# A hybrid attention, retention and ConvFFN layer: sums of the down weights, turned rows and gated rows placed earlier

## The chip, the cores and the metric

The kernel runs on one core of a Trainium2 chip. The metric is the device time of one execution in microseconds. Engines are named as in the profile: PE is TensorE (matmuls and transposes), ACT ScalarE, DVE VectorE, POOL GpSimd, SP SyncE, from whose queue nearly all DMAs are issued.

## What is computed

One layer over 1024 latent tokens of 1024 channels, with 256 context tokens. In the reference's words, cut:

```python
hx = _modulate(_rmsnorm(x, norm1_g[l]), sh1, sc1)
(xq, xk, xv, xrq, xrk, xrv, xrg, xga, xgb) = jnp.split(hx @ w_in[l], IN_OFFSETS, axis=-1)
o_na = _na_latent(grid(xq), grid(xk), grid(xv), kc_na, vc_na, na_rpb[l])
o_ret_x, _, _ = _bi_retention(q_r, k_r, _heads(xrv, RET_HEADS), ...)
o_ret = _ret_output(o_ret_x, xrg)
merged = jax.nn.sigmoid(xga) * (o_na @ w_proj_na) + jax.nn.sigmoid(xgb) * (o_ret @ w_proj_ret)
x = x + g1 * (merged @ w_out)
hx2 = _modulate(_rmsnorm(x, norm2_g[l]), sh2, sc2)
x = x + g2 * _conv_ffn(hx2, w_up[l], conv_w[l], conv_b[l], w_down[l])
return _rmsnorm(x, final_norm_g)
```

All is fp32. The modulation values (`sh1` to `g2`) are silu(c) times `w_ada`.

## The kernel before, in words

**Numbers.** Every operand of a matmul is split into a high and a low part: ACT casts the high part (L86), DVE subtracts it from the source (L87), and a product is three matmuls: high by high (L110), high weight by low operand (L111), low weight by high operand (L112). The function `chain` writes them in this order for one output bank; a chain over 512 channels has 12 matmuls, one over 1024 has 24. A weight block of 128x512 is loaded into a ring of three raw tiles (`rawload`, L91) and split into a ring of six tiles `wc`. Gates, up and down use a scheme of Strassen and Winograd on two by two blocks with seven products (`Seven`): sums of the weight blocks are formed first, on POOL or DVE.

**Order.** Instructions are written as Python loops with generators that yield between pieces; a scheduler then puts each engine's instructions in an order, by priorities, but instructions wrapped in `late` keep their program order. What the engines run is fixed before the launch. Each engine works through its own list in order and waits at an instruction until its operands are there; SP does the same with DMAs, so a store that waits for its tile holds all DMAs behind it.

**Stages**, with their place in the profiled span:

1. Start (0 to about 95 us): norms, modulation, first projections.
2. Neighbourhood attention (95 to 397): a loop over 32 units (head pair by row block) with two extra rounds. In each round one unit computes scores and softmax, the one before it transposes its probabilities (bank `ptp`), splits them into `PT` (L496, L504) and multiplies them with the values into `R` (L511), and the one before that is normalised and stored to `d_ona` (L524). `R`'s two halves are added in L514. Beside it, filler pieces on PE are projection chains of the next pair and gate chains. In each round DVE also multiplies one block of `w_ada` (tile `aw`, one buffer, 512 KB) with silu(c) and sums it (L538); its result is used at stage 4.
3. Retention, head by head, with the mixing of the head before as a second stream (397 to 700), and a tail in which the last head is mixed beside three gate chains (`gate_fill`, to 720).
4. Turn and projection of the attention (720 to 773): the rows `d_ona` are loaded as eight raw tiles `onr` of 128 tokens by 512 channels, PE turns them in 32 transposes of 128x128 into banks `tpn` (L1366), ACT copies each bank as high part of `ona` (L1368), DVE subtracts the low part (L1369). Then 16 chains `pn` of 12 matmuls: output block db by token half, `w_pna[db]` against `ona`. In between POOL and DVE form `hx_sums`, sums of normalised input blocks for the gates, split into `hxT`.
5. Gates (773 to 926): eight units `Gates` of seven steps, 12 matmuls a step, interleaved two steps apart (`interleaved`). A finished bank goes through silu or sigmoid (L1484 on ACT), is multiplied with the retention's output or the projected attention on DVE, and stored to `d_orr` (gated rows), `d_pn` or `d_gate`.
6. pr chains (926 to 1024): 16 chains of 24 matmuls, `w_pret[db]` against the gated rows `orr` of one token half. `orr` of half 0 is loaded and split while the last gates run, one block a step from the last unit's first step on (`n0`), and put where `hx` is no longer read (tags of `hxpool`); half 1 is loaded after the gates. The result is multiplied with a gate and added to the projected attention, `sg` (L1600, L1601).
7. Output projection (1024 to 1137), up (to 1551), down (to 1772).

**The sums of the down weights.** `down_sums` forms, for each of 11 blocks j, four sums of the down weights' quarters for stage 7: four loads of 256 KB (`pj`, L1241), four subtracts on POOL (L1249), four stores to `d_w` (L1251). Before, they are spread: five j in the retention (`ret_sums`, one piece per slot, 8 buffers), four in the gates (one piece in three steps), two among the pr chains (7 buffers).

**`gate1`**, the row of the residual's gate broadcast to 128 partitions, is loaded in the middle of stage 6 (`brow`), used in stage 7.

## Time and profile before

| | |
|---|---|
| runs (us) | 1779.46, 1778.84, 1776.31; median 1778.84 |
| profiled execution, its span (us) | 1772.4; the median of the runs is 6.4 longer |
| granted PE clock | 0.991 |
| busy: PE, DVE, ACT, POOL | 97%, 74%, 48%, 32% |
| DMA, moved in all | 261.62 MB, mean 148 GB/s |

The profile has one time for the profiled execution, its span from the first to the last instruction; the runs' times are taken around the whole execution. In the tables `out<-in` names the tiles without their buffer numbers, and a line number is that of the kernel before. A matmul's duration overlaps with that of the next one (0.39 us long, 0.23 us apart), so on PE the distance between two starts is what counts. A value in brackets is the time an engine stood idle ahead of the row, and what it waited for.

### The profile page before, as it was taken

How to read it: one execution, taken by the hardware profiler on the slowest of the kernel's cores; microseconds unless marked ns; L12 is line 12 of the kernel's file. 1: busy time of each engine (PE TensorE's matmuls, PEld its weight loads, DVE VectorE, ACT ScalarE, POOL GpSimd, SP SyncE). 2: the span in 40 equal slices, each digit the busy share in tenths (PEclk: the TensorE clock that was granted, in tenths of full speed). 3: DMA queues.
4: the chain of work that ended last, by engine and by line, in shares of the span. 5: the costliest groups of instructions: out<-in, count | busy, mean ns of one | idle time of the engine just before them, and what ended most of it. 6: DMA issues, size and time to landing. Idle time of an engine off the chain costs nothing.

```text
span 1772.4 us, 24732 instructions
## 1 busy us (share of the span) xinstructions
PE 1725.5 (97%) x8357; PEld 1429.4 (81%) x8357; DVE 1312.3 (74%) x2458; ACT 851.1 (48%) x1833; POOL 570.9 (32%) x477
## 2 busy tenths in 40 slices
PE   8799999999999999999999999999999999999997
PEld 4588888888888888788877888888888888788886
DVE  5978888765776766777655556889899999876755
ACT  5667666652443444443444323454444444554444
POOL 2610000002334343555412400155455555211444
PEclk9899999999999999999999999999999999999999
DMA  9133334432231212677548733742322332586754
GB/s 357 56 113 120 106 113 134 142 110 104 72 108 48 72 39 65 202 243 241 187 168 278 236 127 137 253 147 91 117 90 89 119 119 90 167 297 191 241 167 151
DMA packets 139552, 261.62 MB, mean 148 GB/s; under 512 B 15872, under 2 KB 28320, under 8 KB 139424
## 3 DMA queue, kind: packets, MB, share of 16 engines
q1 hardware_dynamic: 139424, 260.03, 44.3%
q8 instruction: 66, 1.08, 0.3%
q14 instruction: 62, 0.51, 0.1%
HBM read 187.87 MB, written 69.48 MB: 145 GB/s over the span
## 4 chain that ended last, share of the span: by engine, by line
PE 39%; issue 6%; DVE 5%; DMA 3%; POOL 3%; ACT 1%; SPq 0%; POOLq 0%; DVEq 0%; ACTq 0%
PE u L1374 27%; PE y L1374 4%; PE pr L111 2%; PE pr L112 1%; PE pr L110 1%; PE om L123 1%; PE om L122 1%; PE om L121 1%; DMA raw<-d_orr 1%; DVE wc L87 1%; POOL x L1899 0%; DMA uu<-d_t 0%; DMA ur<-in_w_up 0%; DVE b L1350 0%; POOL pd L1936 0%
## 5 line engine op out<-in xcount | busy, mean ns | idle before, releaser
L1374 PE MATMUL u<-T,wc 128*128 128x512 f32 x960 | 225.7, 391 | 0.6 <-ACT pu L1413 0.3
L1374 PE MATMUL y<-wc,ahl 128*128 128x512 f32 x924 | 212.0, 391 | 2.9 <-DVE wc L87 1.8
L1374 PEld LDWEIGHTS u<-T,wc 128*128 128x128 f32 x960 | 179.4, 188 | 41.5 <-ACT pu L1413 4.2
L1374 PEld LDWEIGHTS y<-wc,ahl 128*128 128x128 f32 x924 | 174.4, 189 | 40.2 <-DVE wc L87 2.5
L87 DVE TENSOR_TENSOR wc<-ur,wc 128x512 fp32r<-128x512 f32 x137 | 125.0, 915 | 62.2 <-ACT wc L86 62.2
L86 ACT CAST wc<-ur 128x512 fp32r<-128x512 f32 x137 | 85.1, 622 | 124.3 <-PE y L1374 71.8
L111 PE MATMUL mm<-low,wc 128*128 128x512 f32 (+1 forms) x328 | 124.0, 378 | 0.0
L1374 PE MATMUL u<-h2a,wc 128*128 128x512 f32 x480 | 112.4, 389 | 0.7 <-DVE pu L1422 0.7
L110 PE MATMUL mm<-hx,wc 128*128 128x512 f32 x264 | 107.4, 407 | 0.3 <-DVE vc L221 0.3
L1374 PEld LDWEIGHTS u<-h2a,wc 128*128 128x128 f32 x480 | 90.0, 188 | 19.9 <-DVE pu L1422 1.2
L112 PE MATMUL mm<-hx,wc 128*128 128x512 f32 x264 | 105.1, 398 | 0.0
L86 ACT CAST wc<-s 128x512 fp32r<-128x512 f32 x80 | 49.6, 621 | 89.7 <-PE u L1374 86.9
L123 PE MATMUL mm<-wc,low 128*128 128x512 f32 (+1 forms) x240 | 91.2, 380 | 0.0
L1513 POOL TENSOR_TENSOR col<-col,bcol 128x32 f32<-128x32 f32 x1 | 0.3, 254 | 281.9 <-DVE aw L538 281.9
L1374 PE MATMUL u<-hxT,wc 128*128 128x512 f32 x384 | 89.6, 389 | 0.0
L87 DVE TENSOR_TENSOR wc<-s,wc 128x512 fp32r<-128x512 f32 x80 | 87.3, 1092 | 3.1 <-ACT wc L86 2.6
L1374 PEld LDWEIGHTS u<-hxT,wc 128*128 128x128 f32 x384 | 72.1, 188 | 15.0
L87 DVE TENSOR_TENSOR wc<-raw,wc 128x512 fp32r<-128x512 f32 x92 | 71.4, 784 | 13.3 <-ACT wc L86 13.2
L121 PE MATMUL mm<-wc,hx 128*128 128x512 f32 x192 | 75.2, 392 | 0.6 <-ACT r L1105 0.6
L122 PE MATMUL mm<-wc,hx 128*128 128x512 f32 x192 | 75.2, 392 | 0.0
L86 ACT CAST wc<-raw 128x512 fp32r<-128x512 f32 x92 | 57.0, 622 | 32.3 <-DMA raw<-in_w_up 5.0
L111 PEld LDWEIGHTS mm<-low,wc 128*128 128x128 f32 x328 | 62.1, 189 | 6.9
(393 smaller groups left out, 4695.7 us busy)
## 6 DMA issues: line engine op xcount, KB each, us to landing
ur<-in_w_up SPq DMA_DIRECT2D x80, 256.0 KB, 3.0
ur<-d_a SPq DMA_DIRECT2D x77, 256.0 KB, 3.0
aw<-in_w_ada SPq DMA_DIRECT2D x32, 512.0 KB, 3.3
pj<-in_w_down SPq DMA_DIRECT2D x44, 256.0 KB, 4.9
d_w<-pj SPq DMA_DIRECT2D x44, 256.0 KB, 2.0
d_a<-sa SPq DMA_DIRECT2D x44, 256.0 KB, 2.0
ur<-d_w SPq DMA_DIRECT2D x44, 256.0 KB, 3.5
d_a<-at SPq DMA_DIRECT2D x33, 256.0 KB, 2.7
```

The costliest lines, as they stand in the source:

```text
L86: act.copy(hi, src)
L87: (lo_eng or vec).tensor_tensor(lo, src, hi.bitcast(F32), ALU.subtract)
L110: pe.matmul(out, wh, xh, start=k == 0, stop=False)
L111: pe.matmul(out, wh, xl, start=False, stop=False)
L112: pe.matmul(out, wl, xh, start=False, stop=k == n - 1)
L121: pe.matmul(out, ah, bh, start=first, stop=False)
L122: pe.matmul(out, ah, bl, start=False, stop=False)
L123: pe.matmul(out, al, bh, start=False, stop=last)
L1374: pe.matmul(out, a, b, start=first and n == 0, stop=last and n == 2, skip_group_check=True)
L1513: pool.tensor_tensor(col[:, 16:48], col[:, 16:48], bcol[:, 16:48], ALU.add)
```

## The change

It has three parts.

**Sums.** All 11 blocks of `down_sums` are formed in the attention's loop. The generator is rewritten: six yields per block, asked for twice a round (68 times for 66 yields), with a ring of three `pj` tiles. Each subtract is tied by `with_vec` to the DVE instruction written before it: it starts only when that one has ended. In the order of after, three subtracts of four are tied to an L514, one to an L538. The sums in the retention, the gates and the pr chains are gone.

**Turned rows.** Four of the eight row blocks (token half 0) are loaded, turned and split in the retention's tail, in banks of its own filler chains (`mm_tile`); the other four behind the first pn chain. `ona` is split by halves, half 0 in a pool of its own. The pn chains go (0,0), (1,0), (0,1), (1,1) and then block by block, with the second weight loaded after the first.

**Gated rows.** The loads of `orr` begin six steps earlier in the gates, so that all eight blocks of half 0 and four of half 1 are fetched there; blocks 4 to 7 of half 0 get a pool of their own (`orl`). The first `w_pret` blocks are loaded in the last three steps of the gates. The pr chains go in the same changed order, the last four blocks of half 1 are loaded first in that stage, and then the second block's weights. `gate1` is loaded at the output projection.

PE's order from the retention's last gate chain (`mm`) over the turn (`tpn`) to the first pn chain, before:

```order
L111 MATMUL mm_8349<-low_715,wc_8262 128x512
L112 MATMUL mm_8349<-hx0_119,wc_8262 128x512
L1366 MATMUL tpn_8429<-ident_76,onr_8411 128x128 x4
L1366 MATMUL tpn_8436<-ident_76,onr_8413 128x128 x4
L1366 MATMUL tpn_8443<-ident_76,onr_8415 128x128 x4
L1366 MATMUL tpn_8450<-ident_76,onr_8417 128x128 x4
L1366 MATMUL tpn_8457<-ident_76,onr_8419 128x128 x4
L1366 MATMUL tpn_8464<-ident_76,onr_8421 128x128 x4
L1366 MATMUL tpn_8471<-ident_76,onr_8423 128x128 x4
L1366 MATMUL tpn_8478<-ident_76,onr_8425 128x128 x4
L110 MATMUL pn_8502<-ona0_8409,wc_8499 128x512
L111 MATMUL pn_8502<-ona1_8410,wc_8499 128x512
```

and after, where `ona00` and `ona01` are the high and low part of half 0:

```order
L111 MATMUL mm_8486<-low_715,wc_8399 128x512
L112 MATMUL mm_8486<-hx0_119,wc_8399 128x512
L110 MATMUL pn_8575<-ona00_4591,wc_8572 128x512
L111 MATMUL pn_8575<-ona01_4592,wc_8572 128x512
L1092 MATMUL tpn_8588<-ident_76,onr_8548 128x128 x3
L112 MATMUL pn_8575<-ona00_4591,wc_8572 128x512
L110 MATMUL pn_8575<-ona00_4591,wc_8572 128x512
L111 MATMUL pn_8575<-ona01_4592,wc_8572 128x512
L112 MATMUL pn_8575<-ona00_4591,wc_8572 128x512
L110 MATMUL pn_8575<-ona00_4591,wc_8572 128x512
L111 MATMUL pn_8575<-ona01_4592,wc_8572 128x512
```

The first pn chain now follows the last gate chain directly, and the transposes left are put into and behind it.

ACT's order at the gates' end, before (`c` is a gate's result, `wr` a gate's weight, `raw` of `wc` a weight `w_pret`, `sg` the merge):

```order
L86 CAST orr_10142<-raw_10144 128x512
L1484 ACTIVATE c_10190<-u_9993 128x512
L86 CAST orr_10169<-raw_10171 128x512
L1484 ACTIVATE c_10215<-c_10215 128x512
L86 CAST orr_10196<-raw_10198 128x512
L86 CAST wc_10245<-raw_10243 128x512
L1484 ACTIVATE c_10238<-c_10238 128x512
L86 CAST wc_10250<-raw_10248 128x512
L1570 ACTIVATE sg_10271<-sg_10271 128x512
L86 CAST orr_10274<-raw_10276 128x512
L86 CAST orr_10280<-raw_10282 128x512
L86 CAST orr_10286<-raw_10288 128x512
```

and after, where `u_10073` is the bank that the last unit's fifth step completes, `wc_10269` and `wc_10293` are the first pr chain's weights, `wc_10272` and `wc_10298` those of the last unit's sixth and seventh step, and `wc_10366` (six rows on) the second pr chain's:

```order
L1496 ACTIVATE c_10213<-c_10213 128x512
L1496 ACTIVATE c_10240<-c_10240 128x512
L1496 ACTIVATE c_10263<-u_10073 128x512
L86 CAST orr_10220<-raw_10222 128x512
L86 CAST wc_10269<-raw_10267 128x512
L86 CAST wc_10272<-wr_10059 128x512
L86 CAST wc_10293<-raw_10291 128x512
L86 CAST wc_10298<-wr_10068 128x512
L1496 ACTIVATE c_10287<-c_10287 128x512
L1588 ACTIVATE sg_10332<-sg_10332 128x512
L1496 ACTIVATE c_10313<-c_10313 128x512
L86 CAST orr_10335<-raw_10337 128x512
```

The cast of the first pr weight, which stood behind the last gates' results, now stands ahead of the last two gate weights, and these behind the silu of `u_10073`. PE has the first two pr matmuls ahead of the last unit's sixth step.

SP's order early in the pr stage, before (`raw` from `in_w_pret` the second pr block's weights):

```order
L1566 DMA sg_10322<-d_pn_62 128x512
L91 DMA raw_10294<-d_orr_63 128x512
L1568 DMA sg_10324<-d_gate_61 128x512
L91 DMA raw_10300<-d_orr_63 128x512
L1566 DMA sg_10337<-d_pn_62 128x512
L91 DMA raw_10306<-d_orr_63 128x512
L91 DMA raw_10312<-d_orr_63 128x512
L1568 DMA sg_10339<-d_gate_61 128x512
L91 DMA raw_10318<-d_orr_63 128x512
L1566 DMA sg_10342<-d_pn_62 128x512
L91 DMA raw_10327<-in_w_pret 128x512
L91 DMA raw_10332<-in_w_pret 128x512
```

and after:

```order
L1499 DMA d_gate_61<-c_10287 128x512
L91 DMA raw_10337<-d_orr_63 128x512
L91 DMA raw_10343<-d_orr_63 128x512
L91 DMA raw_10349<-d_orr_63 128x512
L1584 DMA sg_10359<-d_pn_62 128x512
L1499 DMA d_pn_62<-c_10313 128x512
L91 DMA raw_10355<-d_orr_63 128x512
L1586 DMA sg_10361<-d_gate_61 128x512
L91 DMA raw_10364<-in_w_pret 128x512
L91 DMA raw_10369<-in_w_pret 128x512
```

Four loads of half 1 are left ahead of the second pr block's weights instead of eight, and the first three of them stand behind the store of `c_10287`, the result of the last unit's sixth step.

The diff, cut:

```diff
+    def with_vec(ins):
+
+        prev = next(i for i in reversed(nc.cur_bb.bb.instructions) if i.engine == mybir.EngineType.DVE)
+        tc.add_manual_dep(ins.ins, prev.name, mybir.DependencyInfo(mybir.DependencyClass.Sync, mybir.DependencyReason.DATA))
+
+    NH = NF // 2
+
+    def down_sums():
+        def load(j, n):
+            t = na.tile([P, 512], F32, tag="pj", bufs=3, name="pj")
+            sync.dma_start(t, io["w_down"][n % 2, NH * (n // 2) + j])
+            return t
+
+        def minus(o, x, y):
+            with_vec(late(pool.tensor_tensor(o, x, y, ALU.subtract)))
+
+        for j in range(NH):
+            b0, b1 = load(j, 0), load(j, 1)
+            yield
+            b3 = load(j, 3)
+            minus(b0, b1, b0)
+            yield
+            sync.dma_start(d_w[j, 0], b0)
+            minus(b1, b3, b1)
+            yield
+            sync.dma_start(d_w[j, 2], b1)
+            minus(b3, b3, b0)
+            yield
+            sync.dma_start(d_w[j, 1], b3)
+            b2 = load(j, 2)
+            yield
+            minus(b2, b2, b3)
+            yield
+            sync.dma_start(d_w[j, 3], b2)
+
+    sums = down_sums()
...
+        next(sums, None)
...
         if u1:
             u1.values()
+        next(sums, None)
         piece()
         piece()
-    for _ in pieces:
-        pass
+    for it in (pieces, sums):
+        for _ in it:
+            pass
     pna.release()
...
+    onl = sb("ona0", "left")
+    d_onat = d_ona.rearrange("r j c d -> (r j c) d")
+    ona = [[onl.tile([P, NPAIR, 512], F32R, name=f"ona0{w}") for w in range(2)], None]
+
+    def ona_turn(n, raw, tp):
+        for k in range(NPAIR):
+            pe.transpose(tp[:, k], raw[:, k * P : (k + 1) * P], ident)
+        dst = [t[:, :, n % 4 * P : (n % 4 + 1) * P] for t in ona[n // 4]]
+        act.copy(dst[0], tp)
+        vec.tensor_tensor(dst[1], tp, dst[0].bitcast(F32), ALU.subtract)
 
...
-            if i < NCB + NTB - 3 and (head.h == 0 or i >= NCB):
-                next(ret_sums, None)
...
+        n = 0
         for _ in range(RET_FILL):
             g = gate_load()
-            yield from gate_fill(rt, "kz", 2, *g)
+            for _ in gate_fill(rt, "kz", 2, *g):
+                yield
+                if n % 4 == 1 and n // 4 < 4:
+                    ona_turn(n // 4, rawload(d_onat[n // 4 * P : (n // 4 + 1) * P]), mm_tile().rearrange("p (k t) -> p k t", k=NPAIR))
+                n += 1
 
...
-    for n in range(KB):
+    for n in range(4, NTB):
         raw = g_raw("onr")
         sync.dma_start(raw, d_onat[n * P : (n + 1) * P])
         onr.append(raw)
     while stores:
         sync.dma_start(*stores.pop(0))
-    for n, raw in enumerate(onr):
-        tp = pg.tile([P, NPAIR, P], F32, tag="g", bufs=6, name="tpn")
-        for k in range(NPAIR):
-            pe.transpose(tp[:, k], raw[:, k * P : (k + 1) * P], ident)
-        dst = [ona[w][:, :, n * P : (n + 1) * P] for w in range(2)]
-        act.copy(dst[0], tp)
-        vec.tensor_tensor(dst[1], tp, dst[0].bitcast(F32), ALU.subtract)
...
-    hs = None
-    for db in range(KB):
-        if db % 2 == 0:
-            hs = hx_sums(db // 2)
+    hs, wp = None, {}
+    for n, (db, half) in enumerate(((0, 0), (1, 0), (0, 1), (1, 1), *((db, half) for db in range(2, KB) for half in range(2)))):
+        if n % 4 == 0:
+            hs = hx_sums(n // 4)
             next(hs)
-        wp = [wload(io["w_pna"][db, 0])]
-        for half in range(2):
-            sl_ = slice(half * 512, half * 512 + 512)
-            m = g_ps("pn")
-            mm_a(m, wp, lambda k: ona[0][:, k, sl_], lambda k: ona[1][:, k, sl_])
...
-        if db % 2 == 0:
+        if db not in wp:
+            wp[db] = [wload(io["w_pna"][db, 0])]
+        m = g_ps("pn")
+        mm_a(m, wp[db], lambda k: ona[half][0][:, k], lambda k: ona[half][1][:, k])
+        if n == 0:
+            for i, raw in enumerate(onr):
+                ona_turn(4 + i, raw, pg.tile([P, NPAIR, P], F32, tag="g", bufs=6, name="tpn"))
...
+        if n % 4 == 2:
             next(hs)
...
+    orl = sb("orr", "left")
...
+    PLACES = {(0, 0): (1, 0), (1, 0): (0, 0), (1, 1): (0, KH)}
 
     def orr_raw(half, k):
-        i, kb = (k // KH if half else 1 - k // KH), k % KH + KH * half
-        orr[half, k] = [hxpool.tile([P, 512], F32R, tag=f"{t}{i}{kb}", bufs=1, name="orr") for t in ("high", "low")]
+        if (half, k // KH) in PLACES:
+            i, k0 = PLACES[half, k // KH]
+            orr[half, k] = [hxpool.tile([P, 512], F32R, tag=f"{t}{i}{k0 + k % KH}", bufs=1, name="orr") for t in ("high", "low")]
+        else:
+            orr[half, k] = [orl.tile([P, 512], F32R, name=f"orr{t}{k}") for t in range(2)]
         return orr[half, k], rawload(d_orr[k, :, half * 512 : half * 512 + 512], late)
 
-    gate_sums = down_sums(gr, RET_SUMS, GATE_SUMS)
     steps = interleaved(0, len(gu))
-    n0, fetched = steps.index((len(gu) - 1, 0)), None
+    n0, fetched = steps.index((len(gu) - 1, 0)) - 6, None
+    fetches = [(0, k) for k in range(2 * RH)] + [(1, k) for k in range(KH)]
+    wp_next = []
     for n, (i, k) in enumerate(steps):
         gu[i].step(k)
-        if n % 3 == 1:
-            next(gate_sums, None)
         if fetched:
             split(*fetched[0], fetched[1])
             fetched = None
-        if n0 <= n < n0 + 2 * RH:
-            fetched = orr_raw(0, n - n0)
-    wp0 = [wload(io["w_pret"][0, i]) for i in range(2)]
-    for _ in gate_sums:
-        pass
+        if 0 <= n - n0 < len(fetches):
+            fetched = orr_raw(*fetches[n - n0])
+        if n >= len(steps) - 3 and len(wp_next) < 2:
+            wp_next.append(wload(io["w_pret"][0, len(wp_next)]))
...
-    gate1 = wop.tile([P, D], F32, name="gate1")
...
-    pjp = sb("out_sums", "right")
-    out_sums = down_sums(pjp, GATE_SUMS, NH, 7)
     mg = {}
-    wp_next = wp0
-    for db in range(KB):
-        wp = wp_next
-        if db == 0:
-            merge_load(0, (0,))
-            for k in range(2 * RH):
-                hl, raw = orr_raw(1, k)
-                split(*hl, raw)
-            merge_load(0, (1,))
-        if db + 1 < KB:
-            wp_next = [wload(io["w_pret"][db + 1, i]) for i in range(2)]
-            merge_load(db + 1)
-        if db == 2:
-            brow(0, gate1)
-        for half in range(2):
-            m = g_ps("pr")
-            mm_a(m, wp, lambda k: orr[half, k][0], lambda k: orr[half, k][1])
...
-            if db > 1:
-                next(out_sums, None)
-    pjp.release()
+    wps = {0: wp_next}
+    merge_load(0, (0,))
+    for k in range(KH, 2 * RH):
+        hl, raw = orr_raw(1, k)
+        split(*hl, raw)
+    merge_load(0, (1,))
+    for n, (db, half) in enumerate(((0, 0), (1, 0), (0, 1), (1, 1), *((db, half) for db in range(2, KB) for half in range(2)))):
+        nx = 1 if n == 0 else db + 1
+        if nx < KB and nx not in wps:
+            wps[nx] = [wload(io["w_pret"][nx, i]) for i in range(2)]
+            merge_load(nx)
+        m = g_ps("pr")
+        mm_a(m, wps[db], lambda k: orr[half, k][0], lambda k: orr[half, k][1])
...
+    orl.release()
...
+    gate1 = brow(0, op.tile([P, D], F32, name="gate1"))
```

64 lines of the change are left out of this document (19 added, 45 removed).

## The prediction

> **What bounds the kernel now.** The page's first part says which engine to follow.
>
> ```profile
> span 1772.4 us, 24732 instructions
> PE 1725.5 (97%) x8357; PEld 1429.4 (81%) x8357; DVE 1312.3 (74%) x2458; ACT 851.1 (48%) x1833; POOL 570.9 (32%) x477
> ```
>
> TensorE (PE) has work in 97% of the span, and the change leaves its matmuls and transposes the same in number. So it can only win back time in which PE stood still or ran slowly, and only lose by making PE wait. The waits view of PE lists where it stands; of its rows these lie where the change reaches (the larger ones above them are in the start, which it does not touch):
>
> ```profile
> PE pr L110 <- ACT wc L86: 2.8, 1, 2.8
> PE pn L112 <- DVE wc L87: 2.2, 2, 1.5
> PE pr L110 <- ACT orr L86: 2.1, 3, 1.3
> PE tpn L1366 <- DVE ona L1369: 2.1, 1, 2.1
> PE pr L111 <- DVE orr L87: 1.4, 4, 0.7
> ```
>
> The columns are total, number and longest. Sum: 10.6 us, in two places. The windows view cuts the span there (attention; turn of the rows and pn chains; gates; first pr chains). The columns are PE, PEld, DVE, ACT, POOL busy, then the granted clock and the DMA share:
>
> ```profile
> 95.00:397.00 302.00, 301.04 (x1853) 263.88 (x1851) 230.40 (x643) 193.33 (x566) 0.71 (x3) 1.00 0.39 120
> 720.00:773.00 53.00, 48.74 (x222) 40.23 (x221) 49.85 (x61) 29.85 (x53) 30.03 (x20) 0.97 0.60 187
> 773.00:926.00 153.00, 153.00 (x678) 126.57 (x676) 99.08 (x121) 61.25 (x102) 64.15 (x43) 1.00 0.62 208
> 926.00:950.00 24.00, 17.68 (x55) 11.53 (x54) 12.69 (x18) 10.99 (x18) 2.56 (x2) 0.86 0.79 263
> ```
>
> PE is full in the gates and nearly so in the attention; taking GpSimd (POOL) work and DMAs out of the gates frees nothing that ends last. What can be won lies in 720–773 and 926–950, where the clock is below 1 too. The timeline of PE there shows why:
>
> ```profile
> 720.04 2.78 PE L1366 MATMUL tpn<-ident,onr 128*128 128x128 f32 x24
> 724.87 1.87 PE L1366 MATMUL tpn<-ident,onr 128*128 128x128 f32 x8 [2.05 <-DVE ona L1369]
> 726.40 0.77 PE L110 MATMUL pn<-ona,wc 128*128 128x512 f32 x1
> ...
> 925.99 0.39 PE L1374 MATMUL u<-hx,wc 128*128 128x512 f32 x1
> 929.18 0.50 PE L110 MATMUL pr<-orr,wc 128*128 128x512 f32 x1 [2.80 <-ACT wc L86]
> ...
> 932.63 0.63 PE L112 MATMUL pr<-orr,wc 128*128 128x512 f32 x1
> 933.06 0.48 PE L110 MATMUL pr<-orr,wc 128*128 128x512 f32 x1
> 933.38 0.39 PE L111 MATMUL pr<-orr,wc 128*128 128x512 f32 x1
> 933.61 0.39 PE L112 MATMUL pr<-orr,wc 128*128 128x512 f32 x1
> ```
>
> Matmuls of 128x512 start 0.23 us apart (933.38, 933.61), but 0.43 apart (932.63, 933.06) after the gap of 2.80: for about 3.4 us (929.9 to 933.3) PE does half its pace, which costs 1.7 us on top of the gap. After 2.05 us the 8 transposes, 0.116 each before (2.78 over 24), take 1.53 too: the same.
>
> **A: the turn.** Now 32 transposes run at once, and PE waits for the vector engine (DVE) and ScalarE (ACT) to empty their banks: 2.05, plus 1.7 of half pace, plus the 2.2 of the two pn waits: 5.95 us. After it, 16 transposes stand in the retention's tail, the first pn chain follows the last gate chain, and the other 16 stand in and behind that chain. The four evacuations moved into the tail lie on ACT and DVE, with filler chains on PE above them: nothing, and at worst 4 x 0.62. The later pn weights now come one pair ahead, so I let the 2.2 go. But the 32 transposes also covered something:
>
> ```profile
> 720.28 0.59 ACT L360 COPY gs<-mm 128x512 f32<-128x512 f32 x1 [1.06 <-PE mm L112]
> 720.77 0.62 ACT L86 CAST wc<-raw 128x512 fp32r<-128x512 f32 x1
> ...
> 721.42 1.12 DVE L87 TENSOR_TENSOR wc<-raw,wc 128x512 fp32r<-128x512 f32 x1 [5.11 <-ACT wc L86]
> ```
>
> The first pn weight's cast stands on ACT behind the copy of the last gate chain, which ends at 720.04; the order of after keeps that. With the cover gone, PE waits from 720.04 to 721.39 for the high half and a moment to restart (1.45), and for the low half, 722.1 to 722.5, about 0.35 more. Such a gap may or may not bring the half pace (2.05 did); a quarter of 1.7 is 0.4. A: 5.95 - 2.2 = 3.8 us won, bounds 0 (half pace for certain, and the tail's copies all in the open) and 5.95 (no new wait).
>
> **B: the gated rows and first pr chains.** In 926–950 PE issued 55 matmuls, 12.5 us at 0.227; from 926.2, the end of the gates, to 950.2 that is 24.0 for 12.5: 11.5 us lost, to 6.3 of gaps, two stretches of half pace and restarts. What follows the change is set by ACT's and SyncE's (SP) orders, with these prices:
>
> ```profile
> 921.83 0.59 ACT L1484 ACTIVATE c<-u 128x512 f32<-128x512 f32 x1
> 922.32 0.61 ACT L86 CAST orr<-raw 128x512 fp32r<-128x512 f32 x1
> ```
>
> The DMA view of 900–960 has the median from issue to landing in its last column:
>
> ```profile
> raw<-d_orr SPq DMA_DIRECT2D x15, 256.0 KB, 3.4
> raw<-in_w_pret SPq DMA_DIRECT2D x9, 256.0 KB, 4.1
> ```
>
> The half-0 rows are all on chip by the end of the gates, so the waits of today go. Two new ones come. Call E the end of the last unit's fifth step (two steps of 12 matmuls, 2.73 us each, before the gates' end). In the order of after PE then turns to the first pr chain, whose weight ACT casts only behind the silu of that step's bank (it waits for E) and one more row: 0.24 to start as after 720.04, then 0.49 (921.83 to 922.32), 0.52 and 0.62: E+1.9, and the low half of this and the next weight on DVE puts the stall at 2.3. Half pace, at a gap like the 2.05 above, 0.55 x 1.7 = 0.9: **B1** 3.2. Then the second pr chain's weight: its load shares a ring of three with the four rows of half 1, behind them in SP's order, and these stand behind a store of the last-but-one gate, ready at E + 2.3 + 2.73 + 0.9 of pr rows + 0.69 and 0.62 on DVE and ACT = E+7.2. Rows land at E+7.5+3.4 = 10.9; cast, they free a slot at 12.3 and 13.0; the fourth row lands at 15.7, the weight issued at 13.0 at 16.6 to 17.1 and is cast by about 17.4. PE ends the two steps and the first chain (24 x 0.227 = 5.45) at E + 2.3 + 5.46 + 5.45 = 13.2. **B2** 4.2, plus 1.7 of half pace: 5.9. B: 11.5 - 9.1 = 2.4 won; bounds -2.5 (B1 with the full half pace, B2 a landing of 4.1 later) and 11.5 (neither arises). I take the middle way since every step of it has a row.
>
> Under "TensorE: Matmul & The Clock Gate", Part 1, the Trainium skill has the clock halve only when PE is idle for a window of about 3.4 us. By that rule B1, B2 and the turn would cost no half pace, 3.0 us less. The rows differ: half pace follows gaps of 2.05 and 2.80 here; its length of 3.4 us agrees.
>
> **C: the sums in the attention.** 44 loads of 256 KB, 44 stores and 44 subtracts come into the 302 us in which PE has under 1 us free. DMA there is at 0.39, so the 23 MB (76 GB/s on 120) fit; weights are loaded several units ahead, so a slower load costs nothing. SP now stops at each store for the subtract, and the loads of `aw` behind it come later; their product (L538) has no reader before the turn, but stands in DVE's order. Three subtracts of four start with the end of the sum L514, one with that of L538. The timeline of DVE behind an L514 (210.99), in an iteration of the busier half, and the R matmuls on PE that this leads to:
>
> ```profile
> 211.31 1.22 DVE L538 SCALAR_TENSOR_TENSOR aw<-aw,cs 128x1024 f32<-128x1024 f32 x1
> ...
> 212.45 1.46 DVE L496 TENSOR_TENSOR PT<-ptp,PT 128x512 fp32r<-128x512 f32 x2
> ...
> 215.09 0.29 DVE L504 TENSOR_TENSOR PT<-ptp,PT 128x128 fp32r<-128x128 f32 x1
> ...
> 215.78 1.36 PE L511 MATMUL R<-PT,V 128*128 128x256 f32 x10
> ```
>
> DVE has no idle from L538 to L504, whose end (215.38) is 0.40 ahead of R. So a hold above 0.4 reaches PE. What a subtract lasts, and what POOL does to a DVE cast, is in the groups by line (min/median/max; the two rows of L87 are of 95–397, where POOL is idle, and of 926–1024):
>
> ```profile
> L1249 POOL TENSOR_TENSOR pj<-pj x44: 1286/1296/1751, 407.3 to 1014.1; 128x512 f32<-128x512 f32 x44
> L87 DVE TENSOR_TENSOR wc<-raw,wc x31: 671/686/693, 97.8 to 388.2; 128x512 fp32r<-128x512 f32 x31
> L87 DVE TENSOR_TENSOR wc<-raw,wc x21: 674/691/1774, 929.2 to 1023.6; 128x512 fp32r<-128x512 f32 x21
> ```
>
> The worst hold is 1.774 - 0.69 = 1.09 us, the median none. L538 stands ready when L514 ends, while POOL must first be told, so DVE should mostly be first and POOL the one to wait; then L496 to L504 follow, each with one operand in PSUM. Of 32 iterations about 16 run as tight as this one (the others, from 310 on above all, have idle before L484 and L496). One in eight of those 16 holds paying 1.09 - 0.4 = 0.7 is 1.4, and I take 1.5; bounds 0 (a gain is excluded, since no PE wait leaves) and 11 (all 16 pay).
>
> **D: the rest.** Without the subtracts DVE's casts in the retention, the gates and the pr chains run freer; PE waits for none of them in the list above but those priced, so 0.5 won, bounds 0 and 1. The `gate1` row now loads at the out projection's start, where two banks hold the results of two chains meanwhile (2 x 5.45 us against one transfer): nothing.
>
> Sum: -3.8 - 2.4 + 1.5 - 0.5 = -5.2 us. The profiled span of 1772.4 becomes 1767.2; the median of the runs, 1778.84 (1776.31 to 1779.46), lies 6.4 above the span, so the median becomes **1773.6**. A measurement of this kernel can tell about 0.2% (3.6 us) from no change: the forecast, -0.29%, stands just past that. Its own range is 1771 to 1777.
>
> **Rivals.**
> 1. *Held in the softmax's chain (slower).* POOL wins the start, each subtract holds DVE for the full 1.09, and the 16 tight iterations each bring R 0.7 late: 11.2 us; a second subtract (44 in 33 iterations, so 11 of them have two) finds no slack left in the half of these that is tight: 5.5 x 0.4 more = 2.2. -5.2 - 1.5 + 13.4 = +6.7: 1785.5. It decides from a mean hold of 0.8 (0.4 of slack and 6.7/16). For it: PE has no idle to give in 95–397, and the chain above has none. Against: DVE is ready first, and the median cast beside POOL is not held. The Trainium skill's "SBUF — State Buffer", on the port that the two engines share, lets a DVE instruction with two SBUF inputs and a GpSimd one that reads SBUF exclude each other for a whole instruction; the 1.774 agrees, and by this rule L538 and L87, both of that kind, are the wrong neighbours for the sums.
> 2. *The new waits eat the gain (no change).* B1 and A's gap both bring the half pace, and the second weight lands 2 us later: B 2.3 + 1.7 + 6.2 + 1.7 = 11.9, A wins 2.5: +0.4 - 2.5 + 1.0 = -1.1: 1777.7. For it: 2.05 was enough once; the DMA share is 0.79 in 926–950. Against: the pj loads leave that stretch.
> 3. *They do not arise (much faster).* ACT is ahead and the weights lie there: B keeps 2 of 11.5, -3.8 - 9.5 + 1.0 = -12.3: 1766.5. For it: today's last gate weights are cast long before use. Against: the order of ACT and SP, which fixes both waits.
> 4. *New gaps bring no half pace.* -5.2 - 3.0 = -8.2: 1770.6. Against: the slow rows after 2.05 and 2.80. For it: the new gaps are no longer than the shorter of these, B2's apart. This is the way of the clock rule cited in B.
>
> **Chances.** Forecast 0.42, rivals in order 0.17, 0.20, 0.16, 0.05. The bound of 0.2% lies at 1775.3 and 1782.4. Faster: three quarters of the forecast, rivals 3 and 4, a little of rival 2: 0.55. Same: the rest of the forecast and most of rival 2: 0.26. Slower: rival 1 and a tail: 0.19. The range leaves out the further halves of rivals 1 and 3: 1765.5 to 1785.5.
>
> **What would show it.** Right: no tpn wait of 2 us in PE's waits; a gap of about 1.8 between the last gate chain and the first pn chain; none on orr in the first pr chain; gaps of 2 to 2.5 in the last unit's sixth step and of about 4 ahead of the second pr chain, both on wc; PE busy in 95–397 still over 299. Wrong: R or score matmuls waiting for DVE there (rival 1), a full PE around the gates' end (rival 3), a gap on wc over 6 (rival 2), a clock of 1.00 behind the new gaps (rival 4).

## The result, and the profile after

| | before | changed |
|---|---|---|
| median of the runs (us) | 1777.57 (1773.79 to 1779.46) | 1795.20 (1792.30 to 1798.33) |
| ratio | | 1.0103, 95% interval 1.0086 to 1.0120 |
| profiled span (us), clock | 1772.4, 0.991 | 1790.5, 0.986 |

The change makes the kernel 1% slower; 1773.6 had been forecast, with a range to 1785.5. A second set of runs of the changed kernel gave 1.0083 (1.0061 to 1.0104). Ratios are taken to runs of the kernel before made beside each run (medians 1779.73, 1781.30 and 1778.75 in the experiments). The first profiles of two of the experiments (memsets, first pn weight) had the PE clock at 0.85 and 0.65 throughout, so their stages are read from a second profile.

Where the time went is read by stages, cut at instructions that both kernels have on PE (first transposed probabilities, first state matmul of the retention, end of the last gate chain ahead of the first pn matmul, first gate matmul, first and last matmul of the output projection, last matmul of the up stage). Durations in us, worked out from the timelines:

| kernel | to attention | attention | retention, tail | turn, pn | gates, pr | out | up | down |
|---|---|---|---|---|---|---|---|---|
| before | 116.7 | 281.3 | 322.0 | 53.8 | 251.5 | 92.7 | 432.9 | 221.4 |
| changed | 120.7 | 288.8 | 324.3 | 51.9 | 255.2 | 92.7 | 437.2 | 219.8 |
| changed, again | 120.6 | 289.5 | 324.7 | 51.2 | 255.6 | 92.7 | 436.4 | 219.8 |

16 of the transposes (1.9 us) now stand in the tail, so retention and turn go together: 375.8 before, 376.2 after. The attention has 7.5 us more and gates with pr 3.7. The 4.0 ahead of the attention and the 4.3 in the up stage, with 1.6 given back in the down stage, lie in code that the change does not touch; the experiments speak of them below.

The waits of PE in the changed kernel, total, number and longest, without those of the start:

```profile
PE pr L110 <- ACT wc L86: 10.6, 2, 6.1
...
PE u L1391 <- ACT pu L1425: 2.8, 2, 2.6
PE pn L112 <- DVE wc L87: 2.5, 1, 2.5
PE ptp L500 <- DVE PT L496: 2.0, 2, 1.6
...
PE pn L110 <- ACT wc L86: 1.2, 1, 1.2
PE ptp L493 <- ACT P L482: 1.0, 1, 1.0
```

The wait on `tpn` and those on `orr` are gone, as they should be. In their place stand two waits for a pr weight, longer than all that they replace, two for the first pn weight, and in the attention waits for `PT` that the kernel before did not have. The row on `pu` lies in the up stage.

**In the attention** DVE is held: some of its instructions last longer while a subtract of POOL runs beside them. These are two of its groups in the kernel before, min/median/max in ns (the third, L87, had 693 at most):

```profile
L484 DVE TENSOR_TENSOR st<-st x32: 155/161/163, 114.2 to 385.5; 128x2 f32<-128x2 f32 x32
```
```profile
L538 DVE SCALAR_TENSOR_TENSOR aw<-aw,cs x32: 1214/1218/1227, 117.3 to 374.4; 128x1024 f32<-128x1024 f32 x32
```

and in the changed kernel:

```profile
L87 DVE TENSOR_TENSOR wc<-raw,wc x32: 673/682/1770, 94.9 to 399.4; 128x512 fp32r<-128x512 f32 x32
```
```profile
L538 DVE SCALAR_TENSOR_TENSOR aw<-aw,cs x32: 1212/1216/2125, 121.2 to 385.4; 128x1024 f32<-128x1024 f32 x32
```
```profile
L484 DVE TENSOR_TENSOR st<-st x32: 146/161/1222, 118.1 to 396.7; 128x2 f32<-128x2 f32 x32
```

L484 adds two columns, 128x2, and still lasts up to 1.22 us: the hold lies inside its own duration, so no wait is shown for it. One such place on DVE:

```profile
303.27 1.22 DVE L538 SCALAR_TENSOR_TENSOR aw<-aw,cs 128x1024 f32<-128x1024 f32 x1
...
304.41 1.77 DVE L87 TENSOR_TENSOR wc<-raw,wc 128x512 fp32r<-128x512 f32 x1
306.11 1.22 DVE L484 TENSOR_TENSOR st<-st 128x2 f32<-128x2 f32 x1
307.36 0.17 DVE L485 RECIPROCAL st<-st 128x2 f32<-128x2 f32 x1
307.44 1.26 DVE L496 TENSOR_TENSOR PT<-ptp,PT 128x512 fp32r<-128x512 f32 x2
```

and in the same stretch POOL (two subtracts) and PE:

```profile
304.05 3.26 POOL L1026 TENSOR_TENSOR pj<-pj 128x512 f32<-128x512 f32 x2 [4.91 <-DVE rs L514]
```
```profile
308.17 0.44 PE L500 MATMUL ptp<-ident,P 128*128 128x128 f32 x2 [1.60 <-DVE PT L496]
```

The cast lasts 1.77 instead of 0.69, the small addition 1.22 instead of 0.16, L496 comes 4.17 us behind L538's start instead of 2.24 (294.91 to 297.15 in the kernel before), and PE waits 1.6 us. In all, 17 instructions of DVE in this stage last 0.45 to 1.1 us longer than the median of their group, 12.7 us together; in the kernel before none lasts even 0.1 longer.

What of this reaches PE can be read by comparing the starts of the same matmuls in the two kernels. The changed kernel falls behind by 0.9 us behind a held L480 (127.48, 1.11 instead of 0.17), by 0.8 behind a held cast (163.93), by 0.4 behind an L538 (181.21) and by 0.4 behind an L484 (235.87), by 1.8 at the place shown, and by 0.2 behind each of five held L484 from 349 on: 5.2 of the 7.5 us. Another 1.9 come between 184 and 213, where DVE stands for a load:

```profile
189.48 0.43 DVE L477 CUSTOM_DVE_ANT_0 P<-sl,bias 128x256 f32<-128x256 f32 x1 [2.04 <-DMA bias<-in_na_bias]
```

SP issued this load at 183.38, behind the store of a sum (181.91) and a load of `aw`; in the kernel before, which is 6 us ahead at this place, it was issued at 172.68, and DVE did not wait for it. PE's order of instructions is also another there, so how the 1.9 divide is not shown. The remaining 0.3 lie at the end of the stage.

**At the gates' end** the loads are late. SP around the end of the last unit's fifth step (932.6 is its last matmul's start):

```profile
932.61 0.32 SPq L1499 DMA_DIRECT2D d_pn<-c  x1
933.02 0.38 SPq L91 DMA_DIRECT2D raw<-d_orr  x1
933.50 0.41 SPq L91 DMA_DIRECT2D raw<-in_w_pret  x1
```

and what ACT does with them:

```profile
934.48 0.58 ACT L1496 ACTIVATE c<-u 128x512 f32<-128x512 f32 x1
936.21 0.62 ACT L86 CAST orr<-raw 128x512 fp32r<-128x512 f32 x1 [1.16 <-DMA raw<-d_orr]
936.82 0.62 ACT L86 CAST wc<-raw 128x512 fp32r<-128x512 f32 x1
```

The row (the twelfth that is fetched, so the fourth of half 1) and the first pr weight are issued only behind the store of an earlier result, at the moment when PE needs the weight. PE stands for the weight twice:

```profile
937.49 0.50 PE L110 MATMUL pr<-orr,wc 128*128 128x512 f32 x1 [4.49 <-ACT wc L86]
...
956.43 0.80 PE L110 MATMUL pr<-orr,wc 128*128 128x512 f32 x1 [6.09 <-ACT wc L86]
```

The second weight is late by SP's order:

```profile
944.50 0.32 SPq L1499 DMA_DIRECT2D d_gate<-c  x1
944.91 1.35 SPq L91 DMA_DIRECT2D raw<-d_orr  x3
...
951.87 0.84 SPq L91 DMA_DIRECT2D raw<-in_w_pret  x2
```

The windows show that half pace follows both (clock in the third column from the end):

```profile
937.40:942.00 4.60, 4.51 (x13) 3.43 (x14) 2.66 (x5) 1.70 (x4) 0.00 (x0) 0.63 0.51 159
...
956.00:961.00 5.00, 4.57 (x11) 3.50 (x12) 2.12 (x4) 2.83 (x5) 0.00 (x0) 0.50 1.02 353
```

**At the turn** the first pn weight's low half is late on DVE, and PE with it:

```profile
731.23 6.82 DVE L1374 TENSOR_TENSOR b<-b 128x512 f32<-128x512 f32 x4 [1.18 <-POOL b L1371]
737.97 1.28 DVE L87 TENSOR_TENSOR wc<-raw,wc 128x512 fp32r<-128x512 f32 x2
```
```profile
735.18 0.50 PE L110 MATMUL pn<-ona,wc 128*128 128x512 f32 x1 [1.24 <-ACT wc L86]
...
738.71 0.79 PE L112 MATMUL pn<-ona,wc 128*128 128x512 f32 x1 [2.46 <-DVE wc L87]
739.30 0.63 PE L110 MATMUL pn<-ona,wc 128*128 128x512 f32 x1
739.73 0.63 PE L111 MATMUL pn<-ona,wc 128*128 128x512 f32 x1
```

Four sums for the gates stand ahead of it in DVE's order. They take 6.8 us, and here too DVE is held: each lasts 1.57 to 1.76 us beside POOL's sums L1371, which form their inputs, instead of 0.69. An estimate from these rows is that they would end some 3 us earlier without the holds, ahead of the end of the weight's cast on ACT (735.13), so that the wait of 2.46 would not arise; this was not tried. 1.24 and 2.46 of waits and 2.1 of half pace (ten matmuls in 4.43 us, 0.43 apart) are 5.8 us, nearly the 5.95 that went.

### The profile page after: what moved, and what is told of

It reads as the page before. It is cut to its first block, busy times and chain, and to the rows that moved or that the text cites. A ratio compares the mean times of both kernels' runs of the same rounds, so it can differ in the third digit from the quotient of the medians.

```text
span 1790.5 us, 24780 instructions
## 1 busy us (share of the span) xinstructions
PE 1734.7 (97%) x8357; PEld 1432.8 (80%) x8357; DVE 1300.4 (73%) x2458; ACT 851.3 (48%) x1833; POOL 575.5 (32%) x477
## 4 chain that ended last, share of the span: by engine, by line
PE 75%; DVE 8%; issue 7%; POOL 4%; DMA 3%; ACT 3%; SPq 1%; POOLq 0%; ACTq 0%; DVEq 0%
PE u L1391 27%; PE mm L122 4%; PE y L1391 4%; PE mm L121 4%; PE mm L123 4%; PE mm L112 3%; PE mm L110 3%; PE mm L111 3%; PE R L511 2%; PE pr L110 2%; PE pr L112 2%; PE pr L111 2%; PE ptp L493 1%; PE om L123 1%; PE om L121 1%
## 5 line engine op out<-in xcount | busy, mean ns | idle before, releaser
L87 DVE TENSOR_TENSOR wc<-ur,wc 128x512 fp32r<-128x512 f32 x137 | 125.2, 916 | 62.0 <-ACT wc L86 62.0
L1026 POOL TENSOR_TENSOR pj<-pj 128x512 f32<-128x512 f32 x44 | 70.0, 1592 | 234.4 <-DVE rs L514 108.5
L87 DVE TENSOR_TENSOR wc<-s,wc 128x512 fp32r<-128x512 f32 x80 | 85.8, 1072 | 3.4 <-ACT wc L86 3.1
L87 DVE TENSOR_TENSOR wc<-raw,wc 128x512 fp32r<-128x512 f32 x92 | 73.9, 812 | 9.9 <-ACT wc L86 9.7
L86 ACT CAST wc<-raw 128x512 fp32r<-128x512 f32 x92 | 56.8, 622 | 39.6 <-PE pr L112 11.6
L1400 POOL TENSOR_TENSOR s<-ur 128x512 f32<-128x512 f32 x20 | 34.1, 1705 | 112.6 <-DVE wc L87 79.7
```

What stands on the lines that cost most here:

```text
L86: act.copy(hi, src)
L87: (lo_eng or vec).tensor_tensor(lo, src, hi.bitcast(F32), ALU.subtract)
L1026: with_vec(late(pool.tensor_tensor(o, x, y, ALU.subtract)))
L1400: pin(pool.tensor_tensor(self.s1, self.a21, self.a22, ALU.add))
```

## The experiments

Theory 1: the subtracts on POOL and DVE's instructions with two operands in SBUF hold each other, and that is the attention's loss; the loss at the gates' end and the turn comes from the order of loads and casts. Theory 2, the rival: in the attention it is the 23 MB more of transfers and SP's stops at the stores. The stage durations are in the table at the end of this part. A change of one part alone to the kernel before was only possible with the sums already moved: the turned rows and the held rows take the space that the moved sums leave.

**The sums alone.** The kernel before, with the sums asked for twice a round in the attention and nowhere else:

```diff
+        next(sums, None)
...
             u1.values()
+        next(sums, None)
...
-                next(ret_sums, None)
...
-            next(gate_sums, None)
...
-                next(out_sums, None)
```

> Only the first part of the change: all 44 down-weight sums in the attention; rows turned and gated rows held as before. Theory 1 (the subtracts on POOL and DVE's two-input instructions hold each other, and this reaches R on PE): 95-400 is about 7 us longer than before, the turn and the gates' end keep the waits of before, total 1777.6 + 7 = about 1784.5. Theory 2 (the extra transfers and SP's stops at the stores cost the time): the same total. Chance theory for the up stage (+4.3 there in the changed kernel came from which engine got in first, not from the change): the wait of 2.6 us on pu in the up stage may or may not appear; if part three causes it, it does not.

1788.44 us, ratio 1.0053 (1.0033 to 1.0073). The attention takes 290.6 us, 9.3 more than before; gates and pr 251.6, as before. So the sums alone make up the loss in the attention, and relieving the gates and the pr stage of them brought nothing. It is 9.3 here and not 7.5 because half pace follows the gap at the place shown above: 1.87 us here, with a clock of 0.66 in the 5 us behind it, against 1.60 us and a clock of 1.00 in the changed kernel. The wait of 2.6 us on `pu` in the up stage is here too, without part three. The run does not tell the two theories apart.

**Sums and turned rows; sums and gated rows.**

To the kernel with the sums alone the one adds part two whole, the other part three whole; of each the line that begins it:

```diff
+                if n % 4 == 1 and n // 4 < 4:
```

```diff
+    n0, fetched = steps.index((len(gu) - 1, 0)) - 6, None
```

> Parts one and two: sums in the attention and half the rows turned in the tail; gated rows as before. Theory 1: the turn gains nothing, because the first pn weight's low half on DVE stands behind four hx sums (1.2 + 2.5 us of waits and 1.7 of half pace against 2.1 + 1.7 + 2.2 removed): within 1 us of the kernel with the sums only, about 1784.5. The recorded forecast's step A (3.8 us won) would give 1780.7.

> Parts one and three: sums in the attention, gated rows held by the gates' end; turn as before. Theory 1: the first pr weights wait about 4.5 us and the second about 6 us, 3.7 us more than the waits of before: about 1788. The recorded step B (2.4 won) would give 1782. If part three also causes the wait on pu in the up stage, that wait is here and in no kernel without part three, and the total is about 1792.

With the turned rows 1792.73, ratio 1.0068 (1.0046 to 1.0090); retention with turn 376.7 us against 376.3 with the sums alone: nothing won, as expected. (Gates and pr take 2.2 more in this kernel, without part three: half pace follows a gap of 1.81 us there.) With the gated rows 1792.81, ratio 1.0069 (1.0044 to 1.0095); gates and pr 255.2 against 251.6, where 3.7 more were expected. The wait on `pu` is not in this kernel (0.4 us), so part three does not cause it. Both totals are higher than the expected 1784.5 and 1788, and the intervals of the three totals overlap; the stages tell them apart.

**No subtracts.**

```diff
         def minus(o, x, y):
-            with_vec(late(pool.tensor_tensor(o, x, y, ALU.subtract)))
+            pass
```

> The changed kernel with its 44 subtracts in the attention left out: the loads and stores stay and the raw blocks are stored, so the down weights' sums are not formed. Theory 1 (port): the attention is 7 us shorter than in the changed kernel, as long as before, total 1795.2 - 7 = about 1788. Theory 2 (transfers and SP): it stays 7 us longer than before, total about 1795.

Missed by both theories: 1806.53, ratio 1.0149 (1.0126 to 1.0172). With the subtracts the ties that space SP's loads and stores were gone too, and PE waited ahead of the first scores for a key block:

```profile
PE sl L472 <- DMA kH<-kH: 10.9, 1, 10.9
```

DVE was no longer held, yet the attention took 286.8, with one gap of 2.5 and more waits for `aw` (3.9 us on DVE). That the transfers, spaced by nothing, crowd out the others is the likely reading; it was not tried by itself. The run does not settle what the subtracts cost, but it shows that late loads alone can cost the attention 5.5 us.

**Memsets in place of the subtracts.**

```diff
-            with_vec(late(pool.tensor_tensor(o, x, y, ALU.subtract)))
+            with_vec(late(pool.memset(o, 0.0)))
```

> The changed kernel, each of its 44 subtracts replaced by a memset of the same tile, tied to the same DVE instruction: POOL then writes as much and reads nothing, and the down weights' sums are left out (zeros are stored). Unlike the run without subtracts, SP still stops at each store for POOL. Theory 1 (POOL's reads and DVE's two-input instructions exclude each other): no DVE instruction in the attention is held any more, and the attention (288.8 us from the first transposed probabilities to its end in the changed kernel, 281.3 before) comes back to 282 to 284; total 6 us below the changed kernel, about 1789. Theory 2 (transfers, SP's stops): the attention stays at 287 to 289.

> The kernel with memsets in the place of the 44 subtracts once more, since the profile of the first run fell in a stretch with the PE clock at 0.85. Theory 1: no held DVE instruction, the attention at 281 to 284 us. Theory 2: 287 to 289.

1790.34, ratio 1.0055 (1.0037 to 1.0072), and 1791.07, ratio 1.0057 (1.0037 to 1.0078). The groups of the second profile:

```profile
L1026 POOL MEMSET pj<- x44: 522/527/549, 117.7 to 396.6; 128x512 f32 x44
```
```profile
L484 DVE TENSOR_TENSOR st<-st x32: 155/161/164, 117.2 to 391.5; 128x2 f32<-128x2 f32 x32
```

The longest L484 is back at 164 ns, L538 at 1227, L87 at 693; of all DVE instructions of the stage one alone lasts 0.1 longer than its median, an L480 (0.29 instead of 0.17) that ends with a memset. That a memset is shorter than a subtract (0.53 against 1.30) is not the reason. 18 of the 44 memsets run from start to end inside an L538, and neither is longer for it; in the changed kernel 16 subtracts begin inside an L538, and each lasts 1.58 to 2.34 us instead of 1.30.

The attention takes 284.6: 4.2 us of the 7.5 are gone. That is 0.6 more than theory 1 allowed and 2.4 less than theory 2. 2.5 of the 3.3 left come in the first 25 us, at three places where DVE stands for the load of `aw` (0.72, 0.45 and 1.91), and PE behind it (0.66, 0.49 and 1.37). The last of them:

```profile
139.79 1.23 DVE L538 SCALAR_TENSOR_TENSOR aw<-aw,cs 128x1024 f32<-128x1024 f32 x1 [1.91 <-DMA aw<-in_w_ada]
```
```profile
142.21 0.66 PE L493 MATMUL ptp<-ident,P 128*128 128x128 f32 x4 [1.37 <-DVE rs L514]
```

This load landed 7.0 us after its issue; the median of `aw` is 3.3 in the kernel before. So the rival is right in part: the transfers make loads late, `aw` here, `bias` in the kernels with the subtracts (1.5 to 2.7 us on DVE in all seven, 0.4 here). The holds of the subtracts are the larger part in the changed kernel, 5.2 of the 7.5.

**Another tie.**

```diff
             u1.transp(0)
+        next(sums, None)
         piece()
...
             u1.values()
-        next(sums, None)
```

> The changed kernel with three subtracts of four asked for right behind the split of the transposed probabilities (L496), whose followers on DVE each have an operand in PSUM, instead of behind the sum L514, whose follower is L538. Theory 1: fewer holds, the attention 3 to 5 us shorter than 288.8, total about 1791. Theory 2: no difference in the attention, about 1795.

1792.65, ratio 1.0067 (1.0043 to 1.0091), attention 288.0: 0.8 less, not 3 to 5. The holds only moved. L538 and L87 are free, and L484 takes them:

```profile
L538 DVE SCALAR_TENSOR_TENSOR aw<-aw,cs x32: 1215/1218/1227, 117.3 to 380.4; 128x1024 f32<-128x1024 f32 x32
```
```profile
L484 DVE TENSOR_TENSOR st<-st x32: 151/161/1251, 114.2 to 391.9; 128x2 f32<-128x2 f32 x32
```

13 of the 64 small additions on `st` are held, against 8 in the changed kernel. A tie only fixes where a subtract may begin; here POOL also waited 17.8 us for `pj` loads, and whatever DVE does by then is its neighbour.

**The first pn weight ahead of the hx sums.**

```diff
+        if db not in wp:
+            wp[db] = [wload(io["w_pna"][db, 0])]
         if n % 4 == 0:
             hs = hx_sums(n // 4)
             next(hs)
-        if db not in wp:
-            wp[db] = [wload(io["w_pna"][db, 0])]
```

> The changed kernel with the first pn weight's load and split written ahead of the hx sums, so that on DVE its low half stands ahead of the four sums of 6.8 us in all. If those sums made step A fail: the wait of 2.5 us on that weight and the half pace behind it go, the stretch from the last gate chain to the gates falls from 51.9 to about 48, total about 1791. If the wait on ACT (1.2) alone brings the half pace, it falls to about 50.

> The changed kernel with the first pn weight ahead of the hx sums once more, for a profile at full clock. If the hx sums are what step A overlooked: the wait for the low half falls from 2.5 to below 0.5 and no half pace follows, last gate chain to gates 47 to 49 us instead of 51.9.

1793.63, ratio 1.0070 (1.0045 to 1.0096), and 1791.84, ratio 1.0072 (1.0048 to 1.0096). The wait for the low half falls from 2.46 to 0.51 and no half pace follows; the windows 733 to 750 of this kernel and of the changed one:

```profile
733.00:750.00 17.00, 13.95 (x66) 10.44 (x65) 14.08 (x17) 10.42 (x18) 13.63 (x11) 1.00 0.49 149
```
```profile
733.00:750.00 17.00, 13.30 (x56) 10.45 (x55) 14.33 (x16) 9.89 (x17) 12.53 (x10) 0.80 0.44 134
```

Ten matmuls and transposes more in the same time. But two new waits (0.57 and 0.70) for the turned rows of half 1 come in the third chain, and the stage as a whole is 49.8 us, 2.1 less, not the 3 to 5 expected. The 0.51 are left because the cast itself is held, 1.54 us instead of 0.68. The total hardly moves (1791.84 beside 1792.73 of the changed kernel).

**The pr order in the kernel before.**

The chains go (0,0), (1,0), (0,1), (1,1) and then block by block, as in the changed kernel:

```diff
+    wps = {0: wp0, 1: [wload(io["w_pret"][1, i]) for i in range(2)]}
     merge_load(0, (0,))
+    merge_load(1, (0,))
     for k in range(2 * RH):
         hl, raw = orr_raw(1, k)
```

> The kernel before, with only the order of the pr stage changed: the second block's weights are loaded ahead of the eight rows of half 1, and the first two chains are those of half 0. Nothing is moved into the attention or the gates. If the waits for the rows of half 1 are covered by a second chain of 5.45 us: the 5.4 us of row waits and one stretch of half pace (1.7) go, the gates and pr stages fall from 251.5 to 245 to 247, total 1778 - 6 = about 1772. Rival: the second weights now wait as the rows did (a gap of 4 to 6 ahead of the second chain) and the total stays at 1778.

1775.42, ratio 0.9972 (0.9956 to 0.9987) to 1781.30: faster than both kernels, by 5 us where 6 were expected. Gates and pr take 246.9, within the expected range. The waits on the pr stage's weights and rows, 6.3 us in the kernel before, are

```profile
PE pr L110 <- ACT wc L86: 2.6, 1, 2.6
PE u L1374 <- ACT pu L1413: 2.6, 1, 2.6
...
PE pr L110 <- ACT orr L86: 1.4, 3, 0.6
```

4.0 us on the pr stage are left. The middle row is the wait in the up stage: it stands in this kernel, which moves nothing into the attention or the gates.

**Both.**

The kernel above, and in its pn loop:

```diff
+        wp = [wload(io["w_pna"][db, 0])]
         if db % 2 == 0:
             hs = hx_sums(db // 2)
             next(hs)
-        wp = [wload(io["w_pna"][db, 0])]
```

> The kernel before with the pr order of the eighth run and, in the pn chains, each weight's load and split written ahead of the hx sums. If DVE's order makes the two waits of 0.9 to 1.5 us in the pn chains: they go, 2 us below the eighth run, about 1773. Rival: the hx sums then come late and the gates wait for them: no gain.

1776.51, ratio 1.0000 (0.9982 to 1.0018): the gain of the pr order is still there (246.2), and the turn loses 2.1 (56.3 against 54.2), since two hx sums and the second weight now stand on DVE ahead of the split of the turned rows, each held beside POOL's sums (1.57 to 1.75 us):

```profile
PE tpn L1366 <- DVE ona L1369: 5.4, 1, 5.4
```

**The changed kernel again**, without an edit.

> The changed kernel itself, beside the other runs of this call. If the wait of 2.6 us in the up stage and the longer start are chance, as the other runs suggest, they vary here too; the attention (288.8), the turn (51.9), gates and pr (255.2) should not. Total about 1794.

1792.73, ratio 1.0083 (1.0061 to 1.0104). Attention, turn, gates and pr are within 0.7 us of the first profile of the changed kernel; the wait on `pu` in the up stage is there again.

| kernel | to attention | attention | retention, tail | turn, pn | gates, pr | out | up | down |
|---|---|---|---|---|---|---|---|---|
| sums alone | 118.6 | 290.6 | 321.8 | 54.6 | 251.6 | 92.7 | 437.6 | 220.0 |
| sums, turn | 121.2 | 291.5 | 324.4 | 52.3 | 253.8 | 92.7 | 435.0 | 219.7 |
| sums, gated rows | 119.4 | 289.0 | 321.5 | 54.3 | 255.2 | 92.7 | 435.0 | 221.9 |
| no subtracts | 133.4 | 286.8 | 324.2 | 51.1 | 257.9 | 92.7 | 433.3 | 220.6 |
| memsets, again | 119.8 | 284.6 | 324.0 | 52.3 | 255.8 | 92.7 | 438.9 | 221.8 |
| other tie | 116.7 | 288.0 | 324.4 | 51.9 | 255.9 | 92.7 | 439.0 | 223.0 |
| weight first, again | 120.8 | 289.2 | 324.4 | 49.8 | 256.3 | 92.7 | 436.9 | 223.2 |
| before, pr order | 121.2 | 281.3 | 321.8 | 54.2 | 246.9 | 92.7 | 437.8 | 223.8 |
| before, both | 120.7 | 281.3 | 321.9 | 56.3 | 246.2 | 92.7 | 439.2 | 221.7 |

Three profiles without the sums have 281.3 us of attention, seven with them (the subtracts in place) 288.0 to 291.5. The time to the attention (116.7 to 121.2, the kernel without subtracts apart) and that of the up stage (432.9 to 439.2) vary whatever the kernel, and of all profiles that of the kernel before has the shortest up stage. Of the 18.1 us between the two profiled spans, 11.2 are the attention and the gates with pr; 0.4 the turn; the rest is not shown to come from the change.

## Why the prediction was wrong

Three steps failed, C by 6.0 us, A by 4.2 and B by 6.1. With what was measured their sum is 11.6 us lost instead of 4.7 won.

**What bounds it.** Right: nothing was won outside the two places named. PE's waits show only part of the loss, though: the five delays of 0.2 us behind L484 are in no list of waits.

**Step C, the sums in the attention: 1.5 lost forecast, 7.5 lost** (9.3 with the sums alone). Its bounds of 0 and 11 hold this, but its mechanism does not. It held that "DVE should mostly be first and POOL the one to wait", and that L496 to L504 then follow. POOL did wait for L538 in 16 cases, and no L496 or L504 was held. What the step left out is what else stands behind L538 and L514: the casts L87, the next L538, and the additions and the multiplication on `st`, which last only 0.16 us. In 9 of the 16 cases the waiting subtract then held one of these; the other 8 holds came where POOL began first. Short instructions are held as long as long ones. The step also put late loads at nothing; the one of `bias` belongs to the 1.9 us above.

Rival 1 had the hold, but not its path: it let it reach PE through R, and R waited for nothing; the transposes into `ptp` came late. Its 13.4 us missed the measured 7.5 by as much on the other side, and its 1785.5 is short of the measured 1795.20 as well. The median of the cast beside POOL, quoted against it, said little, since a median does not tell how often a cast meets POOL.

**Step A, the turn: 3.8 won forecast, 0.4 lost.** The wait for the high half came as forecast (1.24 against 1.45). The step put the low half of the weight at 0.35 us behind the high half, as in the kernel before. There DVE had been idle for 5.1 us ahead of that cast; in the order of after four hx sums stand there, held by POOL's. The wait was 2.46 and brought the half pace. The run with the first pn weight ahead of the sums shows this term: it falls to 0.51, and 2.1 us of the stage are won.

**Step B, the gates' end: 2.4 won forecast, 3.7 lost.** Both new waits came, at the places named, and for the reason named; the terms were mis-sized. B1 was 4.49 against 2.3: the bank's silu began 1.5 us after the bank was complete (at 933.0) and not 0.24, behind another gate's result on ACT, and the row that ACT casts next was issued at 933.02 only, so that ACT stood 1.16 us for it. B2 was 6.09 against 4.2: with B1 the store ahead of the rows came at 944.50, 11.5 us behind that moment and not 7.2, and the first row landed 4.7 us after its issue, not 3.4. The half pace and restarts behind both were 4.5 against 2.6, from the starts: 16 matmuls in 5.43 us behind B1 and 13 in 5.70 behind B2, where 0.227 each would be 3.6 and 3.0. Together 15.1 against 9.1, which is the 6 us by which the stage missed.

**Step D** was near: nothing in the gates or pr (251.6 with the sums alone), nothing for `gate1` (out 92.7 in all).

**The base of the sum.** The forecast's sum rested on a profiled execution that was a fast one, with an up stage 4 us shorter than in most. Of the 6.4 us added from span to median 4.6 are that: in the later runs on record a time lies 1.8 us above its own span (1792.30 and 1790.5 for the changed kernel).

**The port rule.** The rule cited with rival 1 (the Trainium skill, "SBUF — State Buffer", on the port that DVE and GpSimd share) has a DVE instruction with two SBUF inputs and a GpSimd one that reads SBUF exclude each other, and a GpSimd instruction that only writes left out of it. The holds of 1.77 and 1.22, and the 18 memsets inside an L538, agree with both halves of it. Two inputs are not the whole condition in this trace: L480, which multiplies one tile in SBUF by a constant, was held as well, 1.11 us by a subtract and 0.29 by a memset.

**The clock rule.** The rule of the Trainium skill cited in step B ("TensorE: Matmul & The Clock Gate", Part 1) would have had no half pace behind 2.46 us; it came there, and behind 1.87 in the kernel with the sums alone. Behind B2 (4.2 forecast, 6.09 measured) the rule does not exclude it, so the 3.0 us that step B and rival 4 took off by it were too much. The length of a gap alone does not settle it in these runs: behind the same wait of 2.60 us on `pu` the clock was 0.61 in the changed kernel and 1.00 in that with sums and turned rows.

## What to carry to other kernels

Before work goes to an engine that is idle, look at what its neighbour does beside it, the shortest instructions too: a hold sits inside durations and not in the list of waits, so compare the median and the largest of each group. Work that was moved off a stage in which PE is full anyway gained nothing. When a stretch that covered a cast or a load is taken away, read the whole order of the engine that owes it. Here the order of the chains alone, with the second weights ahead of the rows, was worth more than all that made room for it.

## What the runs showed of the hardware

Which of POOL and DVE gets in first can decide microseconds far from any change. In the up stage POOL's sum L1389 begins at 1159.46 in the kernel before, and lasts 5.16 us, until seven casts of DVE have ended. In the kernel before with the pr order POOL gets in ahead of the first cast, with three sums one after the other; three of the casts last 1.77 us each instead of 0.68, the seven take 3.3 us longer, and PE waits 2.6 (the wait on `pu`). POOL and then DVE, in the kernel before:

```profile
1159.46 5.16 POOL L1389 TENSOR_TENSOR s<-s,ur 128x512 f32<-128x512 f32 x1 [11.58 <-DMA ur<-in_w_up]
```
```profile
1159.18 4.30 DVE L87 TENSOR_TENSOR T<-uu,T 128x512 fp32r<-128x512 f32 x7
```

and in that with the pr order:

```profile
1159.45 1.61 POOL L1389 TENSOR_TENSOR s<-s,ur 128x512 f32<-128x512 f32 x1 [10.59 <-DMA ur<-in_w_up]
```
```profile
1159.83 7.59 DVE L87 TENSOR_TENSOR T<-uu,T 128x512 fp32r<-128x512 f32 x7
```

DVE's and POOL's orders are the same in both at this place; the first cast begins 0.28 us ahead of POOL's sum in the one and 0.38 behind it in the other, and 3.3 us hang on it. What lets an engine in is not shown: in the kernel before, POOL's sum has also begun when the second cast does (1159.78), and yet it waits for all seven.
